# A third pair of raw weight buffers in the feed-forward stages, with two of the four weight sums made in place of raw blocks

## The chip, the cores and the metric

The kernel runs on one core of one Trainium2 chip. The metric is the device time of one execution in microseconds. The core has a matrix engine (TensorE, PE in the profile, with its weight loads as PEld), VectorE (DVE), ScalarE (ACT), GpSimd (POOL), and DMA queues that SyncE (SP) feeds. Each engine works through its own list of instructions in order; between engines an instruction waits on semaphores. TensorE reads its operands from SBUF and adds into PSUM; DVE and ACT read PSUM.

## The reference

The kernel computes two "macaron" layers over T = 528 tokens (16 learned tokens and 512 given ones) of width D = 1024. A layer is a feed-forward half step, a mixer (retention and differential attention) and another feed-forward half step:

```
def swiglu(x, w_gate, w_up, w_down):
    return (jax.nn.silu(x @ w_gate) * (x @ w_up)) @ w_down

for l in range(DEPTH):
    h = h + 0.5 * swiglu(rmsnorm(h, ffn1_norm[l]), ffn1_w_gate[l], ffn1_w_up[l], ffn1_w_down[l])
    proj = rmsnorm(h, mix_norm[l]) @ w_in[l]
    ...
    h = h + jnp.concatenate([y_ret, y_diff], axis=-1) @ w_out[l]
    h = h + 0.5 * swiglu(rmsnorm(h, ffn2_norm[l]), ffn2_w_gate[l], ffn2_w_up[l], ffn2_w_down[l])
return rmsnorm(h, final_norm)[:, N_META:]
```

All of it is in float32, and the inner width of the feed-forward is 2816, that is 22 blocks m of 128.

## The kernel before

**Stages.** The span holds four feed-forward stages, about 30 to 400 us, 700 to 1055, 1055 to 1415 and 1717 to 2094, with a mixer behind the first and behind the third. Each stage is one call of `ffn`, with a pool of SBUF buffers of its own. It works in chunks: the gate and up products of some blocks, then the down projection of those blocks (`FFN_CHUNKS`, `ffn_steps`). The change touches the gate and up products alone.

**Products.** A float32 operand is split into a high part (hi, by ACT, line 108) and the rest (lo, `in - hi`, by DVE, line 109), and each product is made of three matmuls of such parts. The first two blocks of a stage are plain (`plain`; their results leave PSUM on lines 542 and 544). From block 2 on, gate and up of one block are made as one 2x2 Strassen-Winograd product (a "pair"): seven products P1 to P7 of 12 matmuls each, 264 columns wide (256 in the last stage), all issued on line 496. A stage has 20 pairs, the kernel 80.

**Weights of a pair.** Two DMAs bring two raw tiles of 512 KB: `top` (blocks a11, a12) and `bot` (a21, a22). `sums` makes S1 = a21 + a22 (DVE, line 129), S3 = a21 + a11 (DVE, line 130), S2 = S1 + a11 (DVE, line 132) and S4 = S2 + a12 (POOL, line 133), into two tiles `ws0` (S2, S3) and `ws1` (S1, S4). Four splits follow: g1 of `top`, g2 of `ws0`, y of a22 (`yhi`, `ylo`), g3 of `ws1`. The results are named `whi`/`wlo` or `xhi`/`xlo`, by the pool that they lie in. P1 and P2 use g1, P6 and P7 use g2, P5 and P3 use g3, P4 uses y. Raw tiles come from one ring of `RAW_BUFS = 4` tiles (`wraw`), that is two pairs; a DMA into one waits until its last reader is done.

**Results of a pair.** In PSUM, P1, P6, P5 and P3 share bank a of a tile `pm`, P7 and P4 its bank c, P2 lies in a tile `pa`. ACT copies bank a three times (line 455, `rc`): u1 behind P1, u2 behind P6, u4 behind P5. DVE then makes the sums in a tile `gu`: line 469 (P2 + u1), line 474 (bank c + u4, behind P5), lines 476 and 477 (behind P3), line 480 (bank c + u2, behind P4), line 481 (times the gate), and the split of the result into `hh` (ACT, line 551) and `hl` (DVE, line 552). As waits go by the tile, a product waits for every reading of its `pm` tile that stands before it: P6 for the copy u1, P7 for u2, P3 for line 474, P4 for line 476.

**Order.** `rounds` asks for P5(n), P1(m), P2(m), P3(n), P6(m), P4(n), P7(m), n being m - 1, and calls `W.step()` after each for a piece of the next weights. The order in which each engine gets its instructions is then set by a scheduler that runs over the program with a timeline of its own.

Of the kernel before, what the change touches and what calls it, by code (L numbers as in the profile page):

```python
# [8 lines left out]
F32 = mybir.dt.float32  # L9
F32R = mybir.dt.float32r  # L10
AF = mybir.ActivationFunctionType
ALU = mybir.AluOpType
# [3 lines left out]
T = 528  # L16
# [47 lines left out]
class Weights:  # L64


    def __init__(self, nc, pool, plan, ahead, dma_ahead):
        self.nc, self.pool, self.plan = nc, pool, plan
        self.ahead, self.dma_ahead = ahead, dma_ahead
        self.raw, self.parts = {}, {}  # L70
        self.n_dma = self.n_split = self.n_used = 0
        self.extra, self.turn = None, 0
        self.gen, self.hold = None, True

    def raw_tile(self):
        return self.pool.tile([128, 1024], F32, tag="wraw", name="wraw", bufs=RAW_BUFS)

    def start(self):
# [9 lines left out]
    def advance_dma(self, upto):  # L88
        nc = self.nc
        while self.n_dma < min(upto, len(self.plan)):  # L90
            srcs, n, kind = self.plan[self.n_dma]
            self.raw[self.n_dma] = [self.raw_tile() for _ in srcs]
            for t, src in zip(self.raw[self.n_dma], srcs):
                nc.sync.dma_start(out=t[:, :n], in_=src)
            self.n_dma += 1
# [15 lines left out]
    def sums(self, i):  # L111

        nc = self.nc
        self.advance_dma(i + 1)
        top, bot = self.raw.pop(i)
        a11, a12, a21, a22 = (t[:, c] for t in (top, bot) for c in (slice(0, 512), slice(512, 1024)))
        S = [self.extra.tile([128, 2 * 528], F32, tag=f"ws{k}", name=f"ws{k}") for k in range(2)]
        s2, s3, s1, s4 = (t[:, 512 * k:512 * k + 512] for t in S for k in range(2))
        g1 = self.parts_tile(True)
        ops = self.parts[i] = {}  # L120

        def put(names, parts):
            for k, name in enumerate(names):
                ops[name] = tuple(p[:, 512 * k:512 * k + 512] for p in parts)

        self.split(g1, top)
        put(("A11", "A12"), g1)
        yield
        nc.vector.tensor_tensor(out=s1, in0=a21, in1=a22, op=ALU.add)
        nc.vector.tensor_tensor(out=s3, in0=a21, in1=a11, op=ALU.add)  # L130
        yield
        nc.vector.tensor_tensor(out=s2, in0=s1, in1=a11, op=ALU.add)  # L132
        nc.gpsimd.tensor_tensor(out=s4, in0=s2, in1=a12, op=ALU.add)  # L133
        yield
        g2 = self.parts_tile(True)
        self.split(g2, S[0][:, 0:1024])
        put(("S2", "S3"), g2)
        yield
        g4 = [self.extra.tile([128, 528], F32R, tag="y" + p, name="y" + p, bufs=2) for p in ("hi", "lo")]
        self.split([p[:, 0:512] for p in g4], a22)  # L140
        put(("A22",), g4)
        yield
        g3 = self.parts_tile(True)
        self.split(g3, S[1][:, 0:1024])
        put(("S1", "S4"), g3)

    def advance_split(self, upto):
# [59 lines left out]
def trunk(ctx, tc, hT, gains, wgu, wd, win, wout, gnw, sublnw, lam, ret_cs, diff_cs, dtab, mask, out):  # L207
    nc = tc.nc
# [7 lines left out]
    for l in range(DEPTH):  # L216
        for f in range(2):
# [5 lines left out]
            for what, *args in ffn_steps(stage_kind(l, f)):  # L223
                if what == "gu":
                    m, = args
# [208 lines left out]
    def ffn(l, f, mode, g_next, kind):  # L434
        with tc.tile_pool(name=f"ffn{l}{f}", bufs=1, reuse_waits="tile") as pool:
            W.extra, W.turn, W.hold = pool, 3, False
            rr = cols(r, mode)
            w = mode[2] // 2
            state, hidden, room = {}, {}, {}

            def scratch(m):

                if m == "t":
                    return pool.tile([128, 1056], F32, tag="gu", name="xt", bufs=2)
                if m < 4:
                    tag = f"h{'hl'[m % 2]}{6 + m // 2}"
                    return pool.tile([128, T], F32, tag=tag, name=tag)
                i = m // 2 - 2
                if i not in room:
                    room[i] = pool.tile([128, 2 * T], F32, tag=f"ws{i}", name=f"ws{i}")  # L450
                return room[i][:, m % 2 * T:m % 2 * T + T]

            def copy(src):
                t = pool.tile([128, 264], F32, tag="rc", name="rc", bufs=5)[:, :w]
# [121 lines left out]
            def down(ab, final):  # L576
                c0, c1 = ab
                if final:
                    n = KF - 1
                    rounds((("P5", n), ("P3", n), ("P4", n)))  # L580
                    act_table(LNEXP)
                srcs = [hidden.pop(m) for m in range(c0, c1)]
                W.hold = final
                for i, (m, md) in enumerate(down_order(kind, final)):
                    P = project(md, srcs, ("pm", "pa")[i % 2])
                    nc.vector.scalar_tensor_tensor(
                        out=P, in0=P, scalar=0.5, in1=cols(r, md), op0=ALU.mult, op1=ALU.mult
                    )
                    nc.vector.tensor_tensor(out=cols(h[m], md), in0=cols(h[m], md), in1=P, op=ALU.add)
                    if not final:  # L590
                        W.step()
                        continue
                    post_h(m, g_next, md, kind, scratch)
                    if g_next == 3 * DEPTH and m == KD - 1:
                        finish(md)
# [415 lines left out]
    for k in PAIRED:  # L1011
# [8 lines left out]
        out=ident, in_=ident, pattern=[[-1, 128]], compare_op=ALU.is_equal, fill=0.0, base=0,  # L1020
# [12 lines left out]
    for l in range(DEPTH):  # L1033
        last = l == DEPTH - 1
        ffn(l, 0, FULL, 3 * l + 1, "mix")
        if l == 0:
            lambdas()
        mix(l, LAST if last else FULL)
        ffn(l, 1, LAST if last else FULL, 3 * l + 3, "last" if last else "pairs")
# [99 lines left out]
```

## Time and profile before

| what | value |
|---|---|
| time of three runs | 2098.67, 2098.49, 2093.8 us, median 2098.49 us |
| time of the profiled execution | 2096.26 us |
| its span, first to last instruction | 2094.5 us |
| mean granted clock of TensorE | 0.992 |
| TensorE busy | 2006.8 us, 96% |
| DVE busy | 1573.0 us, 75% |
| ACT busy | 965.7 us, 46% |
| POOL busy | 410.0 us, 20% |

TensorE is the engine that nearly always works. What the other engines do shows in the time only where TensorE waits for them. The rows give starts and durations in microseconds; the modelled end of a matmul lies about 0.28 us behind its start, while the starts lie 0.12 us apart, so matmuls overlap in the rows.

### The profile page before, as it was taken

What the parts mean: (1) busy time and instruction counts of PE and PEld (TensorE: products, weight loads), DVE (VectorE), ACT (ScalarE), POOL (GpSimd) and SP (SyncE); (2) the same over time, 40 slices, a digit from 0 to 9 for tenths busy, and PEclk for the clock granted to TensorE, in tenths of its full rate; (3) what the DMA queues carried; (4) which work ended last, traced back from release to release, by engine and by line L of the source; (5) the groups of instructions that cost most, each with busy time, mean ns of one, the idle gap of its engine ahead of it and who ended that gap; (6) DMA issues with size and microseconds to landing.
All of it is one profiled execution on the core that took longest, in us unless ns stands there. A gap on an engine that the chain in (4) does not pass through costs nothing. (4 is left out here: it accounts for less than half of the span.)

```text
span 2094.5 us, 36936 instructions
## 1 busy us (share of the span) xinstructions
PE 2006.8 (96%) x15238; PEld 1930.9 (92%) x15238; DVE 1573.0 (75%) x2292; ACT 965.7 (46%) x1506; POOL 410.0 (20%) x286
## 2 busy tenths in 40 slices
PE   6999999999999999999989999999999999999996
PEld 5899999999999999999989999999888879898995
DVE  8867857668777886867698587766778789696765
ACT  5533525445446552543565254344554465353443
POOL 4100000344343100100110010004434331010002
PEclk8999999999999999999999999999999999999998
DMA  4241323321112242232323223233212223333231
GB/s 153 91 131 52 121 81 95 120 68 64 57 61 90 89 123 70 95 129 68 94 102 102 91 91 116 67 99 114 66 62 62 70 81 101 101 101 121 80 104 49
DMA packets 57656, 190.08 MB, mean 91 GB/s; under 512 B 7056, under 2 KB 9104, under 8 KB 57488
## 3 DMA queue, kind: packets, MB, share of 16 engines
q1 hardware_dynamic: 56464, 186.66, 27.4%
q8 instruction: 119, 1.95, 0.4%
q10 hardware_dynamic: 1024, 1.08, 0.3%
q14 instruction: 49, 0.40, 0.1%
HBM read 184.53 MB, written 2.10 MB: 89 GB/s over the span
## 5 line engine op out<-in xcount | busy, mean ns | idle before, releaser
L133 POOL TENSOR_TENSOR ws<-ws,wraw 128x512 f32<-128x512 f32 x80 | 118.7, 1484 | 1101.0 <-DVE ws L132 931.8
L108 ACT ACTIVATE whi<-wraw 128x1024 fp32r<-128x1024 f32 (+1 forms) x180 | 184.8, 1032 | 274.7 <-PE pm L280 149.2
L496 PE MATMUL pm<-XH,xhi 128*128 128x264 f32 (+1 forms) x848 | 243.2, 287 | 11.0 <-DVE gu L474 5.4
L496 PE MATMUL pm<-XH,xlo 128*128 128x264 f32 (+1 forms) x848 | 240.5, 284 | 0.0
L496 PE MATMUL pm<-XL,xhi 128*128 128x264 f32 (+1 forms) x848 | 240.4, 283 | 0.0
L496 PE MATMUL pm<-XH,whi 128*128 128x264 f32 (+1 forms) x752 | 215.6, 287 | 6.8 <-DVE gu L474 6.6
L496 PE MATMUL pm<-XH,wlo 128*128 128x264 f32 (+1 forms) x752 | 213.1, 283 | 0.0
L496 PE MATMUL pm<-XL,whi 128*128 128x264 f32 (+1 forms) x752 | 213.0, 283 | 0.0
L109 DVE TENSOR_TENSOR wlo<-wraw,whi 128x1024 fp32r<-128x1024 f32 (+1 forms) x148 | 186.2, 1258 | 25.1 <-ACT whi L108 24.4
L280 PE MATMUL pm<-XH,whi 128*128 128x264 f32 (+1 forms) x768 | 181.1, 304 | 9.1 <-DVE ra L668 8.2
L280 PE MATMUL pm<-XL,whi 128*128 128x264 f32 (+1 forms) x768 | 178.7, 301 | 0.0
L280 PE MATMUL pm<-XH,wlo 128*128 128x264 f32 (+1 forms) x768 | 178.7, 302 | 0.0
L496 PEld LDWEIGHTS pm<-XH,xhi 128*128 128x128 f32 x848 | 159.5, 188 | 16.3 <-DVE gu L474 7.9
L496 PEld LDWEIGHTS pm<-XH,xlo 128*128 128x128 f32 x848 | 159.8, 188 | 0.3
L496 PEld LDWEIGHTS pm<-XL,xhi 128*128 128x128 f32 x848 | 159.9, 189 | 0.0
L496 PEld LDWEIGHTS pm<-XH,whi 128*128 128x128 f32 x752 | 141.4, 188 | 9.8 <-DVE gu L474 8.9
L496 PEld LDWEIGHTS pm<-XH,wlo 128*128 128x128 f32 x752 | 141.7, 188 | 0.2
L496 PEld LDWEIGHTS pm<-XL,whi 128*128 128x128 f32 x752 | 141.7, 188 | 0.0
L280 PEld LDWEIGHTS pm<-XH,whi 128*128 128x128 f32 x768 | 123.8, 189 | 16.9 <-issue 4.1
L108 ACT ACTIVATE xhi<-ws 128x1024 fp32r<-128x1024 f32 x84 | 88.9, 1058 | 103.7 <-PE pm L496 37.1
L108 ACT ACTIVATE whi<-ws 128x1024 fp32r<-128x1024 f32 x76 | 80.5, 1059 | 108.9 <-PE pm L496 45.2
L280 PEld LDWEIGHTS pm<-XL,whi 128*128 128x128 f32 x768 | 123.4, 189 | 4.7
(268 smaller groups left out, 6083.6 us busy)
## 6 DMA issues: line engine op xcount, KB each, us to landing
wraw<-in_wgu SPq DMA_DIRECT2D x175, 512.0 KB
wraw<-in_wd SPq DMA_DIRECT2D x66, 512.0 KB
wraw<-in_win SPq DMA_DIRECT2D x56, 512.0 KB
wraw<-in_wd SPq DMA_DIRECT2D x32, 384.0 KB
wraw<-in_wout SPq DMA_DIRECT2D x16, 512.0 KB
slabs<-in_hT SPq DMA_DIRECT2D x8, 264.0 KB
out_y<-slabs SPq DMA_DIRECT2D x8, 256.0 KB
acc1h<-in_dtab SPq DMA_DIRECT2D x4, 264.0 KB
```

Source lines behind the costliest of these rows:

```text
L108: self.nc.scalar.activation(out=hi, in_=t, func=AF.Copy)
L109: (eng or self.nc.vector).tensor_tensor(out=lo, in0=t, in1=hi.bitcast(F32), op=ALU.subtract)
L133: nc.gpsimd.tensor_tensor(out=s4, in0=s2, in1=a12, op=ALU.add)
L280: nc.tensor.matmul(out=ps[:, o:o + c1 - c0], lhsT=a, rhs=b[:, c0:c1], start=start and n == 0, stop=stop and n == 2,)
L496: nc.tensor.matmul(out=out_, lhsT=p[:, s], rhs=q, start=k == 0 and n == 0 and what in ("P1", "P2", "P7"), stop=k == 3 and n == 2, skip_gro ...
```

## The change

Every third pair is fetched into a ring of its own, `xraw`, of two tiles, in the stage's pool. The tiles `ws0` and `ws1` become one tile `ws` (S2, S3). S1 is written over a21 and S4 over a22, both in the raw tile `bot`. So a22 has to be split (y) before S4 overwrites it: `yhi` is issued before the sums and `ylo` ahead of POOL's S4, which now waits for it; and g3 is split from `bot`, which stays in use until then. The number of matmuls, splits, sums and DMAs stays the same. Lines move down by four in most places: 108 becomes 112, 109 becomes 113 (`ylo` 139), 129/130/132/133 become 136/135/138/143, 455 becomes 459, 469/474/476/480/481 become 473/478/480/484/485, 496 becomes 500, 542 becomes 546, 552 becomes 556.

```diff
-    def raw_tile(self):
+    def raw_tile(self, own=False):
+        if own:
+            return self.extra.tile([128, 1024], F32, tag="xraw", name="xraw", bufs=2)
         return self.pool.tile([128, 1024], F32, tag="wraw", name="wraw", bufs=RAW_BUFS)
...
             srcs, n, kind = self.plan[self.n_dma]
-            self.raw[self.n_dma] = [self.raw_tile() for _ in srcs]
+            own = kind == "pair" and self.extra is not None
+            self.n_pairs += own
+            self.raw[self.n_dma] = [self.raw_tile(own and self.n_pairs % 3 == 0) for _ in srcs]
...
-        S = [self.extra.tile([128, 2 * 528], F32, tag=f"ws{k}", name=f"ws{k}") for k in range(2)]
-        s2, s3, s1, s4 = (t[:, 512 * k:512 * k + 512] for t in S for k in range(2))
+        S = self.extra.tile([128, 1024], F32, tag="ws", name="ws")
+        s2, s3 = S[:, 0:512], S[:, 512:1024]
...
         yield
-        nc.vector.tensor_tensor(out=s1, in0=a21, in1=a22, op=ALU.add)
+        g4 = [self.extra.tile([128, 528], F32R, tag="y" + p, name="y" + p, bufs=2) for p in ("hi", "lo")]
+        nc.scalar.activation(out=g4[0][:, 0:512], in_=a22, func=AF.Copy)
         nc.vector.tensor_tensor(out=s3, in0=a21, in1=a11, op=ALU.add)
+        nc.vector.tensor_tensor(out=a21, in0=a21, in1=a22, op=ALU.add)
         yield
-        nc.vector.tensor_tensor(out=s2, in0=s1, in1=a11, op=ALU.add)
-        nc.gpsimd.tensor_tensor(out=s4, in0=s2, in1=a12, op=ALU.add)
+        nc.vector.tensor_tensor(out=s2, in0=a21, in1=a11, op=ALU.add)
+        nc.vector.tensor_tensor(
+            out=g4[1][:, 0:512], in0=a22, in1=g4[0][:, 0:512].bitcast(F32), op=ALU.subtract
+        )
+        put(("A22",), [p[:, 0:512] for p in g4])
+        nc.gpsimd.tensor_tensor(out=a22, in0=s2, in1=a12, op=ALU.add)
         yield
         g2 = self.parts_tile(True)
-        self.split(g2, S[0][:, 0:1024])
+        self.split(g2, S)
         put(("S2", "S3"), g2)
         yield
-        g4 = [self.extra.tile([128, 528], F32R, tag="y" + p, name="y" + p, bufs=2) for p in ("hi", "lo")]
-        self.split([p[:, 0:512] for p in g4], a22)
-        put(("A22",), g4)
-        yield
         g3 = self.parts_tile(True)
-        self.split(g3, S[1][:, 0:1024])
+        self.split(g3, bot)
         put(("S1", "S4"), g3)
```

The scratch tiles of the last down projection, which lay in the `ws` buffers, now lie in those of `yhi` and `ylo`.

The first place is on DVE in the first chunk of the first stage, from the sum behind one pair's P4 (`gu_612`, bank c of `pm_575`) on. Before:

```order
L480 TENSOR_TENSOR gu_612<-pm_575,rc_669 128x264
L481 SCALAR_TENSOR_TENSOR gu_612<-gu_612 128x528
L109 TENSOR_TENSOR ylo_694<-wraw_387,yhi_693 128x512
L552 TENSOR_TENSOR hl3_824<-gu_612,hh3_823 128x528
L109 TENSOR_TENSOR xlo_788<-ws0_734,xhi_787 128x1024
L474 TENSOR_TENSOR gu_752<-pm_713,rc_859 128x264
L130 TENSOR_TENSOR ws0_862<-wraw_578,wraw_577 128x512
```

The same place of the change, where the pair is `gu_618` and the next one `gu_747`:

```order
L484 TENSOR_TENSOR gu_618<-pm_576,rc_673 128x264
L485 SCALAR_TENSOR_TENSOR gu_618<-gu_618 128x528
L139 TENSOR_TENSOR ylo_622<-wraw_386,yhi_621 128x512
L478 TENSOR_TENSOR gu_747<-pm_709,rc_854 128x264
L556 TENSOR_TENSOR hl3_823<-gu_618,hh3_822 128x528
L135 TENSOR_TENSOR ws_730<-wraw_502,wraw_501 128x512
L473 TENSOR_TENSOR gu_874<-pa_839,rc_875 128x264
L136 TENSOR_TENSOR wraw_502<-wraw_502 128x512
L481 TENSOR_TENSOR gu_874<-gu_874,r_71 128x264
L480 TENSOR_TENSOR gu_747<-pm_709,r_71 128x264
L113 TENSOR_TENSOR wlo_676<-wraw_386,whi_675 128x1024
```

The sum behind P5 (line 474, now 478) stood behind a 1024-wide split and now stands right behind `ylo`. The raw tile `bot` of this pair (`wraw_387`, now `wraw_386`) was read for the last time by `ylo_694`, and is now read until `wlo_676`.

The second place is the pair after that one. On DVE the change has there:

```order
L484 TENSOR_TENSOR gu_747<-pm_709,rc_802 128x264
L139 TENSOR_TENSOR ylo_751<-wraw_502,yhi_750 128x512
L485 SCALAR_TENSOR_TENSOR gu_747<-gu_747 128x528
L113 TENSOR_TENSOR xlo_787<-ws_730,xhi_786 128x1024
L556 TENSOR_TENSOR hl4_950<-gu_747,hh4_949 128x528
L478 TENSOR_TENSOR gu_874<-pm_838,rc_981 128x264
L135 TENSOR_TENSOR ws_857<-xraw_579,xraw_578 128x512
L113 TENSOR_TENSOR xlo_805<-wraw_502,xhi_804 128x1024
```

POOL's S4 into `wraw_502` may start behind `ylo_751`. On ACT at that place, before:

```order
L455 ACTIVATE rc_987<-pm_843 128x264
L108 ACTIVATE xhi_992<-wraw_715 128x1024
L455 ACTIVATE rc_1009<-pm_971 128x264
L108 ACTIVATE whi_955<-ws1_863 128x1024
L266 ACTIVATE gu_880<-gu_880 128x528
L455 ACTIVATE rc_1059<-pm_971 128x264
```

And on ACT in the change, where the next pair's tile is `pm_965`:

```order
L459 ACTIVATE rc_981<-pm_838 128x264
L112 ACTIVATE xhi_804<-wraw_502 128x1024
L112 ACTIVATE xhi_985<-wraw_711 128x1024
L459 ACTIVATE rc_1002<-pm_965 128x264
L459 ACTIVATE rc_1056<-pm_965 128x264
L272 ACTIVATE gu_874<-gu_874 128x528
```

The copy u1 (`rc_1009`) stood ahead of the split that reads S4 (`whi_955`); now u1 (`rc_1002`) stands behind that split (`xhi_804`) and another.

The third place is the start of the first stage on DVE, around the results of the two plain blocks (`gu` on line 542, now 546). Before:

```order
L413 SCALAR_TENSOR_TENSOR r_71<-sq_265,sq_266 128x528
L109 TENSOR_TENSOR wlo_450<-ws0_403,whi_449 128x1024
L542 TENSOR_TENSOR gu_349<-pm_207,r_71 128x528
L542 TENSOR_TENSOR gu_485<-pm_361,r_71 128x528
L109 TENSOR_TENSOR wlo_482<-ws1_404,whi_481 128x1024
L130 TENSOR_TENSOR ws0_522<-wraw_358,wraw_357 128x512
```

And in the change:

```order
L113 TENSOR_TENSOR wlo_452<-ws_402,whi_451 128x1024
L419 SCALAR_TENSOR_TENSOR r_71<-sq_265,sq_266 128x528
L113 TENSOR_TENSOR wlo_468<-wraw_275,whi_467 128x1024
L135 TENSOR_TENSOR ws_520<-xraw_357,xraw_356 128x512
L546 TENSOR_TENSOR gu_348<-pm_207,r_71 128x528
L546 TENSOR_TENSOR gu_483<-pm_360,r_71 128x528
```

A split of g3 (`wlo_482`, now `wlo_468`) and the first sum of the third pair moved ahead of the two results; the split of g2 (`wlo_450`, now `wlo_452`) moved ahead of line 413, now 419.

## Rows read from the trace of the kernel before

**Rows 1.** The page, busy time of TensorE.
```profile
PE 2006.8 (96%) x15238; PEld 1930.9 (92%) x15238; DVE 1573.0 (75%) x2292; ACT 965.7 (46%) x1506; POOL 410.0 (20%) x286
```
**Rows 2.** Waits of PE: waiting line, whom for: us in total, times, longest.
```profile
PE pm L496 <- DVE gu L474: 12.0, 16, 1.7
...
PE pm L496 <- DVE gu L476: 4.0, 7, 0.9
PE pm L496 <- DVE gu L542: 3.7, 2, 2.0
PE pa L496 <- DVE gu L469: 3.1, 3, 1.5
...
PE pm L496 <- ACT rc L455: 1.3, 5, 0.3
```
**Rows 3.** Timeline of PE around one such wait: start, duration, instruction, idle before.
```profile
100.42 0.28 PE L496 MATMUL pm<-XL,xhi 128*128 128x264 f32 x1
101.09 0.39 PE L496 MATMUL pm<-XH,whi 128*128 128x264 f32 x1 [0.39 <-DVE gu L474]
101.32 0.28 PE L496 MATMUL pm<-XH,wlo 128*128 128x264 f32 x1
```
**Rows 4.** PE by windows: us, busy (matmuls), clock, DMA share, GB/s.
```profile
200.00:250.00 50.00, 48.86 (x388) 1.00 0.30 106
250.00:300.00 50.00, 50.00 (x414) 1.00 0.37 117
```
**Rows 5.** Timeline of DVE, first stage, first chunk.
```profile
89.74 0.43 DVE L474 TENSOR_TENSOR gu<-pm,rc 128x264 f32<-128x264 f32 x1
...
96.37 0.43 DVE L480 TENSOR_TENSOR gu<-pm,rc 128x264 f32<-128x264 f32 x1 [0.56 <-PE pm L496]
96.91 0.90 DVE L481 SCALAR_TENSOR_TENSOR gu<-gu 128x528 f32<-128x528 f32 x1
97.73 0.68 DVE L109 TENSOR_TENSOR ylo<-wraw,yhi 128x512 fp32r<-128x512 f32 x1
98.52 0.71 DVE L552 TENSOR_TENSOR hl<-gu,hh 128x528 fp32r<-128x528 f32 x1
99.47 1.23 DVE L109 TENSOR_TENSOR wlo<-ws,whi 128x1024 fp32r<-128x1024 f32 x1 [0.24 <-ACT whi L108]
100.61 0.43 DVE L474 TENSOR_TENSOR gu<-pm,rc 128x264 f32<-128x264 f32 x1
```
**Rows 6.** That chunk: PE, PEld, DVE, ACT, POOL busy, then as above.
```profile
78.00:110.00 32.00, 29.87 (x241) 29.45 (x242) 28.45 (x43) 16.59 (x26) 3.87 (x3) 1.00 0.29 95
```
**Rows 7.** Waits of DVE for weights.
```profile
DVE ws L130 <- DMA wraw<-in_wgu: 32.3, 29, 3.4
```
**Rows 8.** Timeline of DVE, first stage, second chunk.
```profile
203.74 0.69 DVE L130 TENSOR_TENSOR ws<-wraw 128x512 f32<-128x512 f32 x1 [1.52 <-DMA wraw<-in_wgu]
...
209.19 1.71 DVE L109 TENSOR_TENSOR ylo<-wraw,yhi 128x512 fp32r<-128x512 f32 x1
```
**Rows 9.** Timeline of PE around a copy u2.
```profile
180.89 0.28 PE L496 MATMUL pa<-XH,whi 128*128 128x264 f32 x1
181.41 0.39 PE L496 MATMUL pm<-XH,xhi 128*128 128x264 f32 x1 [0.23 <-ACT rc L455]
```
**Rows 10.** Timeline of DVE at the first stage's start.
```profile
53.73 1.31 DVE L542 TENSOR_TENSOR gu<-pm,r 128x528 f32<-128x528 f32 x2
56.06 1.23 DVE L109 TENSOR_TENSOR wlo<-ws,whi 128x1024 fp32r<-128x1024 f32 x1 [1.02 <-ACT whi L108]
57.20 0.68 DVE L130 TENSOR_TENSOR ws<-wraw 128x512 f32<-128x512 f32 x1
```
**Rows 11.** Timeline of POOL: S4 near 51 us, and in the second chunk.
```profile
51.16 3.78 POOL L133 TENSOR_TENSOR ws<-ws,wraw 128x512 f32<-128x512 f32 x1 [8.70 <-DVE ws L132]
...
209.06 1.29 POOL L133 TENSOR_TENSOR ws<-ws,wraw 128x512 f32<-128x512 f32 x1 [9.49 <-DVE ws L132]
```
**Rows 12.** Timeline of ACT: one 1024-wide high part.
```profile
102.92 1.06 ACT L108 ACTIVATE whi<-ws 128x1024 fp32r<-128x1024 f32 x1 [0.84 <-PE pm L496]
```

More of the change, by code (lines that the diff above doesn't have):

```diff
@@ L71, in __init__ @@
         self.n_dma = self.n_split = self.n_used = 0
-        self.extra, self.turn = None, 0
+        self.extra, self.turn, self.n_pairs = None, 0, 0
         self.gen, self.hold = None, True
-    def raw_tile(self):
+    def raw_tile(self, own=False):
+        if own:
+            return self.extra.tile([128, 1024], F32, tag="xraw", name="xraw", bufs=2)
         return self.pool.tile([128, 1024], F32, tag="wraw", name="wraw", bufs=RAW_BUFS)
@@ L438, in ffn @@
             w = mode[2] // 2
-            state, hidden, room = {}, {}, {}
+            state, hidden = {}, {}
             def scratch(m):
@@ L447, in scratch @@
                     return pool.tile([128, T], F32, tag=tag, name=tag)
[L448 to L451, printed above, removed]
+                tag = "y" + ("hi", "lo")[m % 2]
+                return pool.tile([128, T], F32, tag=tag, name="xb", bufs=2)
             def copy(src):
```

## The prediction

> **What bounds the kernel now.** I read the page's busy times first, then the waits of TensorE, then single waits in the timelines, then what VectorE does in the same stretch. TensorE is busy for 2006.8 of 2094.5 us [rows 1], so a change can only win back what TensorE loses by waiting, and can only cost where it makes TensorE wait. The change touches the gate and up products, line 496. There TensorE waits 12.0 us for line 474 (sixteen times, ahead of P3), 4.0 for line 476 (seven times, ahead of P4), 3.7 for line 542 (twice, at stage starts), 3.1 for line 469 (three times) and 1.3 for the copies on line 455 (five times) [rows 2]. That is 24.1 us in 33 waits.
>
> A shown wait is less than what it costs. Undisturbed, 414 matmuls start in 50 us, one each 0.121 us [rows 4]. Around a wait shown as 0.39 us the starts lie 0.67 and then 0.23 us apart [rows 3]; against 0.121 each that loses 0.55 and 0.11, together 0.66, so 0.27 more than is shown. With 33 x 0.27 = 8.9 the ceiling of what can come back is 33.0 us. The windows say the same in the rough: a window of the second chunk has 388 matmuls instead of 414 [rows 4], 3.2 us lost in 50.
>
> **VectorE is nearly as full as TensorE in these stretches.** From 78 to 110 us it is busy for 28.45 of 32 us [rows 6]. A pair takes 100.61 - 89.74 = 10.87 us there [rows 5], so VectorE works 9.66 us per pair. TensorE's 84 matmuls need 10.2. VectorE has about half a microsecond to spare per pair, and everything depends on what stands where in its list.
>
> **Line 474 moves up.** In the first chunk line 480 starts behind P4 at 96.37, and then 481, `ylo`, `hl` and a split of 1.14 us (99.47 to 100.61) stand ahead of line 474, which ends at 101.04 [rows 5]; P3 should have started at 100.42 + 0.12 [rows 3]. The change puts 478 right behind `ylo` in one pair of two (first place in the order): by the starts of the same rows it then begins 98.52 - 96.37 = 2.15 us behind line 484's start and ends after 2.6, where 28 matmuls, 3.4 us, now stand between P4 and P3 in TensorE's list. In the next pair (second place) the split and `hl` are still ahead of it, which takes some 3.8 us and 0.43 for itself, but 47 matmuls, 5.7 us, stand there. So both kinds of pair have 0.8 us or more in hand. These sixteen waits cost 12.0 + 16 x 0.27 = 16.3 us. I take back 13, since the first pair of each stage stays tight. Bounds: 0, if other lateness fills the gap, and 16.3.
>
> **The weights no longer come late.** VectorE waits 32.3 us for raw weights on line 130 [rows 7], in the second chunks of every stage above all. At 203.74 it has stood for 1.52 us [rows 8], and lines 469 and 476 queue behind it, for which P2's and P4's banks wait. Before, `bot` is in use for 24 rows of VectorE's list, from line 130 to `ylo`, with two pairs of buffers. Now it is 15 rows, to the low part of g3, with three. The DMA then starts at least one pair earlier, 10 us, against a wait that is at most 3.4 us long [rows 7]. The waits on lines 476 and 469 cost 4.0 + 3.1 + 10 x 0.27 = 9.8 us, of which I take back 8. Bounds: 0 and 9.8.
>
> **P7 directly behind P6.** P7 must wait for the copy u2 of P6's result. In the order of before P7 stands directly behind P6 (with fewer than three other matmuls between) in 4 of 80 pairs, in the change in 17. Such a place reads 180.89 to 181.41 [rows 9], 0.52 us where 0.12 is due, with 0.1 behind it as above, so 0.5 us. 13 x 0.5 = +6.5. It costs nothing where TensorE would have waited just after anyway, so the bounds are 0 and +6.5.
>
> **The first stage starts later.** Line 546 now stands behind one more split, 57.20 - 56.06 = 1.14 us, and behind line 135, 0.68 us [rows 10]. That is 1.8 us, and up to 1.0 more if the split waits for ACT as it did at 56.06 [rows 10]. TensorE waits for this line already [rows 2], so all of it counts: +2. The other three stages have no more work ahead of that line. Bounds: 0 and +2.8.
>
> **S4 meets VectorE.** At 209.06 POOL's S4 runs for 1.29 us [rows 11], and `ylo`, which starts in it, takes 1.71 us [rows 8] instead of 0.68 [rows 5]: 1.03 us lost on VectorE. Now S4 is released by the end of `ylo`, so in nearly every pair the next sum or split of VectorE with two SBUF operands can lose this. That hurts where 478 is still to come behind it, in the 15 or so pairs ordered like the second place. They have about a microsecond in hand, so I count a third of a microsecond for each: +5. Bounds: 0, and 80 x (1.03 - 0.5 to spare) = +42.
>
> **Sum.** -13 - 8 + 6.5 + 2 + 5 = -7.5 us. The profiled execution took 2096.26 us, so 2088.8. The median of the runs shown, 2098.49, lies 2.2 us higher; I leave the prediction at **2089 us**. A difference within 0.3% of the median (6.3 us, so from 2092.2 to 2104.8) can hardly be told from no change.
>
> **Rival 1, VectorE becomes the limit (no measurable change).** If S4 takes 1.03 us from VectorE in every pair, of which before has some already (0.90 on line 481, where `hl`, as wide, takes 0.71 [rows 5], so 0.2), VectorE needs 9.66 + 0.8 = 10.5 us per pair against 10.2. Then line 478 comes late although it stands earlier, the 13 us stay lost, and only the weights' 8 come back: 2096.3 - 8 + 6.5 + 2 = 2097 us. For it speaks that the lock is seen in the trace; against it, that a PSUM reading operation, 478, often stands right behind `ylo`, and that VectorE's list has slack in the chunks that no longer wait for weights. The Trainium skill, "SBUF — State Buffer", section "🔬 SBUF: two separate sides", says that VectorE and GpSimd share a port pair as an exclusive lock, held for a whole instruction by whichever starts first, with VectorE operations on two SBUF operands among those that need it. The 1.71 us agree with it.
>
> **Rival 2, the gains without the costs (clearly faster).** If u2's copy and the collisions fall into time that TensorE had to spare, and the first pairs gain too: 2096.3 - 16.3 - 9.8 + 2 = 2072 us.
>
> **Rival 3, S4 is starved and a copy comes late (slower).** Near 51 us S4 took 3.78 us [rows 11], while VectorE ran operations on SBUF back to back until line 542, at 53.73 [rows 10], which reads PSUM. At the second place `ylo` is followed by three such operations without a break until 478. There ACT has `xhi_804`, which reads S4, then another split, each 1.06 us [rows 12], ahead of the copy u1, for which P6 waits. P6 stands 59 matmuls, 7.2 us, behind P4. `ylo` ends about 1.3 us behind P4, or 2.3 if VectorE runs a microsecond late; the splits and the copy take 2.5; so S4 has 3.4 or 2.4 us. At 1.29 nothing happens; at 3.78 P6 waits up to 1.3 us. In 15 pairs this costs 20 us and brings -13 - 8 + 6.5 + 2 + 20 = +7.5, 2104 us; with ten more pairs in which g3's parts come late for P5 it is 2117. Against it: S4 usually took 1.29 us.
>
> **Rival 4, the weights still come late.** A DMA into `xraw` has the same queue as all others, and one that waits for its buffer holds the next. Then the 8 us do not come, nor, with VectorE late, half of the 13: 2096.3 - 6.5 + 6.5 + 2 + 5 = 2103 us. Against it: 10 us of lead against 3.4.
>
> **Chances.** My forecast 0.42 (2081 to 2094, of which 0.38 is faster by over 0.3%), rival 1 0.23 (0.03 faster, 0.18 the same, 0.02 slower), rival 2 0.15 (faster), rival 3 0.13 (slower), rival 4 0.07 (0.05 the same, 0.02 slower). So faster 0.56, same 0.27, slower 0.17. The range goes from below rival 2, 2068, to rival 4 and the mild end of rival 3, 2104. The forecast's own range is 2081 to 2094.
>
> **What would show it.** Right: VectorE's waits for raw weights at line 135 near 0; the waits on 478 below 4 us and on 480 and 473 below 2; some 18 waits on the copies of line 459 with 6 us in all as lost; the first line 546 about 2 us later. Wrong: many waits on line 459 of a microsecond, ahead of P6, with S4 above 2.5 us (rival 3); waits on 478 as many as before, with VectorE without pauses (rival 1); waits for DMA on line 135 (rival 4).

## The result, and the profile after

The changed kernel takes 2122.45 us (median of 4 runs, 2121.13 to 2124.05) against 2098.58 us before: a ratio of 1.0114, 95% interval 1.0099 to 1.013. It is 24 us slower, where 2089 us had been forecast. The profiled execution took 2122.54 us, 26.3 us more than the one before, and its span is 2120.5 us.

The page's busy times, and POOL's S4 in the view of groups by line (busy time, mean of one, idle before and what ended it):

```profile
PE 2018.9 (95%) x15238; PEld 1940.5 (92%) x15238; DVE 1565.0 (74%) x2292; ACT 961.6 (45%) x1506; POOL 449.1 (21%) x286
...
L143 POOL TENSOR_TENSOR wraw<-ws,wraw 128x512 f32<-128x512 f32 x54 | 107.2, 1985 | 772.2 <-DVE ylo L139 572.1 <-DVE ws L138 168.5 <-ACT hh L555 26.2
L143 POOL TENSOR_TENSOR xraw<-ws,xraw 128x512 f32<-128x512 f32 x26 | 50.3, 1934 | 356.4 <-DVE ylo L139 328.3 <-PE pa L522 18.5 <-DVE ws L138 9.6
```

The 80 S4 take 107.2 + 50.3 = 157.5 us of POOL, 1.97 us each, where before they took 118.7 us, 1.48 each. Eighteen of them last over 2.6 us (before, four).

TensorE's waits in the changed kernel, of the gate and up products (line 500) and of the down projection (286), to be read beside [rows 2]:

```profile
PE pm L500 <- ACT rc L459: 16.7, 27, 2.8
...
PE pm L500 <- DVE gu L546: 7.9, 2, 6.3
PE pm L500 <- DVE gu L478: 7.2, 7, 1.3
...
PE pa L500 <- DVE xlo L113: 2.9, 6, 0.9
PE pa L286 <- ACT whi L112: 2.5, 3, 0.9
...
PE pa L500 <- ACT whi L112: 1.6, 4, 0.6
...
PE pm L500 <- DVE gu L480: 0.7, 1, 0.7
PE pa L500 <- ACT xhi L112: 0.6, 1, 0.6
PE pa L286 <- DVE xlo L113: 0.6, 1, 0.6
```

With the 0.27 us that a wait costs beyond what is shown, the account is:

| TensorE waits for | before | after | difference | forecast |
|---|---|---|---|---|
| line 474, now 478 | 12.0 + 16 x 0.27 = 16.3 | 7.2 + 7 x 0.27 = 9.1 | -7.2 | -13 |
| 476 and 469, now 480 and 473 | 9.8 | 0.7 + 0.27 = 1.0 | -8.8 | -8 |
| the copies, 455, now 459 | 1.3 + 5 x 0.27 = 2.7 | 16.7 + 27 x 0.27 = 24.0 | +21.3 | +6.5 and +5 |
| 542, now 546 | 3.7 + 0.5 = 4.2 | 7.9 + 0.5 = 8.4 | +4.2 | +2 |
| parts of weights, for P2 and the down projection | 0.7 + 0.3 = 1.0 | 8.2 + 15 x 0.27 = 12.3 | +11.3 | none |

That is +20.8 us of the 26.3. About 2 more are the lower clock at the start, shown below. Two single waits of before that are gone, on line 544 and of tile `pa` for a copy, gave back 1.8 us and aren't in the table, so some 5 us are left without an account.

The mechanism can be read at one place, the second one of the order lists in the section on the change. VectorE's timeline there (start, duration, instruction, idle before and what ended it):

```profile
101.65 0.42 DVE L484 TENSOR_TENSOR gu<-pm,rc 128x264 f32<-128x264 f32 x1
101.99 0.67 DVE L139 TENSOR_TENSOR ylo<-wraw,yhi 128x512 fp32r<-128x512 f32 x1
102.59 0.69 DVE L485 SCALAR_TENSOR_TENSOR gu<-gu 128x528 f32<-128x528 f32 x1
103.21 1.21 DVE L113 TENSOR_TENSOR xlo<-ws,xhi 128x1024 fp32r<-128x1024 f32 x1
104.35 0.69 DVE L556 TENSOR_TENSOR hl<-gu,hh 128x528 fp32r<-128x528 f32 x1
104.97 0.42 DVE L478 TENSOR_TENSOR gu<-pm,rc 128x264 f32<-128x264 f32 x1
106.23 0.69 DVE L135 TENSOR_TENSOR ws<-xraw 128x512 f32<-128x512 f32 x1 [0.84 <-POOL wraw L143]
```

POOL's timeline, this S4 and two others:

```profile
49.70 5.87 POOL L143 TENSOR_TENSOR wraw<-ws,wraw 128x512 f32<-128x512 f32 x1 [5.38 <-ACT XH L333]
...
102.80 3.39 POOL L143 TENSOR_TENSOR wraw<-ws,wraw 128x512 f32<-128x512 f32 x1 [6.74 <-DVE ylo L139]
...
125.08 3.88 POOL L143 TENSOR_TENSOR wraw<-ws,wraw 128x512 f32<-128x512 f32 x1 [6.74 <-DVE ylo L139]
```

ACT's timeline, and then TensorE's, behind that S4 (two 1024-wide high parts stand in one row):

```profile
103.87 0.37 ACT L459 ACTIVATE rc<-pm 128x264 f32<-128x264 f32 x1
106.22 2.01 ACT L112 ACTIVATE xhi<-wraw 128x1024 fp32r<-128x1024 f32 x2 [1.98 <-POOL wraw L143]
108.14 0.37 ACT L459 ACTIVATE rc<-pm 128x264 f32<-128x264 f32 x1
```

```profile
107.63 0.28 PE L500 MATMUL pm<-XL,whi 128*128 128x264 f32 x1
108.56 0.39 PE L500 MATMUL pm<-XH,xhi 128*128 128x264 f32 x1 [0.64 <-ACT rc L459]
...
130.38 0.39 PE L500 MATMUL pm<-XH,xhi 128*128 128x264 f32 x1 [2.84 <-ACT rc L459]
```

S4 is released when `ylo` ends, 102.66, and starts at 102.80. VectorE's next three operations (485, a split, `hl`) read two SBUF operands each and follow one another without a gap. S4 ends at 106.19, which is 1.22 us behind the start of 478, the first operation that reads PSUM; alone it takes 1.29. ACT has waited 1.98 us for it, makes two splits, and only then the copy u1, for which P6 waits at 108.56. The S4 of 125.08 does the same, with 2.84 us at TensorE. At 97.73 in [rows 5] `ylo` waited for nothing of that kind, since S4 had started behind line 132, with a pause and then 480, which reads PSUM, next on VectorE.

Counted by the starts of all matmuls (start to start less 0.12 us, from 0.1 us on), the waits of tile `pm` that a copy ended cost TensorE 2.7 us in 7 places before and 23.1 in 37 after. In 15 places it is P6 that waits for u1, and ACT's work ahead of that copy begins with the end of an S4; these cost 11.2 us, of which two cost 3.0 each (before, no such place). In 18 places P7 waits for u2, mostly directly behind P6; these cost 10.1 us (before, 4 with 1.7). The other 4 cost 1.8. The copies are not all that S4 holds up: waits of `pa` for parts of weights that lead back to the end of an S4 through ACT's and VectorE's lists cost another 9.8 us in 21 places (before, none).

The start of the first stage, VectorE's timeline (to be read beside [rows 10]), and TensorE by windows:

```profile
52.62 1.21 DVE L113 TENSOR_TENSOR wlo<-ws,whi 128x1024 fp32r<-128x1024 f32 x1
53.76 0.69 DVE L419 SCALAR_TENSOR_TENSOR r<-sq 128x528 f32<-128x528 f32 x1
56.69 1.23 DVE L113 TENSOR_TENSOR wlo<-wraw,whi 128x1024 fp32r<-128x1024 f32 x1 [2.24 <-ACT whi L112]
57.83 0.68 DVE L135 TENSOR_TENSOR ws<-xraw 128x512 f32<-128x512 f32 x1
58.43 1.31 DVE L546 TENSOR_TENSOR gu<-pm,r 128x528 f32<-128x528 f32 x2
```

```profile
56.00:59.00 3.00, 0.00 (x0) 0.78 0.78 265
59.00:62.00 3.00, 2.72 (x12) 0.50 0.70 270
62.00:66.00 4.00, 4.00 (x26) 0.69 0.00 0
```

Line 546 starts at 58.43 instead of 53.73. TensorE waits 6.3 us, and then the granted clock is 0.50, the 1.2 GHz level, and 0.69 in the next window: 38 matmuls start in 7 us, where 58 fit at 0.121 us.

### The profile page after: what moved, and what is told of

Its sections match the earlier page's. It is cut to its first block, busy times and chain, and to the rows that moved or that the text cites. A ratio compares the mean times of both kernels' runs of the same rounds, so it can differ in the third digit from the quotient of the medians.

```text
span 2120.5 us, 36818 instructions
## 1 busy us (share of the span) xinstructions
PE 2018.9 (95%) x15238; PEld 1940.5 (92%) x15238; DVE 1565.0 (74%) x2292; ACT 961.6 (45%) x1506; POOL 449.1 (21%) x286
## 3 DMA queue, kind: packets, MB, share of 16 engines
q10 hardware_dynamic: 1024, 1.08, 0.3%
## 5 line engine op out<-in xcount | busy, mean ns | idle before, releaser
L112 ACT ACTIVATE whi<-wraw 128x1024 fp32r<-128x1024 f32 (+1 forms) x196 | 199.8, 1033 | 273.1 <-PE pm L286 131.4
L143 POOL TENSOR_TENSOR wraw<-ws,wraw 128x512 f32<-128x512 f32 x54 | 107.2, 1985 | 772.2 <-DVE ylo L139 572.1
L113 DVE TENSOR_TENSOR wlo<-wraw,whi 128x1024 fp32r<-128x1024 f32 (+1 forms) x164 | 203.4, 1244 | 29.0 <-ACT whi L112 28.5
L459 ACT ACTIVATE rc<-pm 128x264 f32<-128x264 f32 (+1 forms) x240 | 90.9, 381 | 144.8 <-PE pm L500 144.4
L500 PEld LDWEIGHTS pm<-XL,whi 128*128 128x128 f32 x752 | 142.3, 189 | 0.0
L590 DVE SCALAR_TENSOR_TENSOR pm<-pm,r 128x528 f32<-128x528 f32 (+2 forms) x49 | 34.2, 698 | 130.8 <-PE pm L286 130.8
L112 ACT ACTIVATE xhi<-wraw 128x1024 fp32r<-128x1024 f32 (+1 forms) x98 | 99.7, 1028 | 68.5 <-DMA wraw<-in_wd 17.0
```

The costliest lines, as they stand in the source:

```text
L112: self.nc.scalar.activation(out=hi, in_=t, func=AF.Copy)
L113: (eng or self.nc.vector).tensor_tensor(out=lo, in0=t, in1=hi.bitcast(F32), op=ALU.subtract)
L143: nc.gpsimd.tensor_tensor(out=a22, in0=s2, in1=a12, op=ALU.add)
L459: nc.scalar.activation(out=t, in_=src, func=AF.Copy)
L500: nc.tensor.matmul(out=out_, lhsT=p[:, s], rhs=q, start=k == 0 and n == 0 and what in ("P1", "P2", "P7"), stop=k == 3 and n == 2, skip_gro ...
L590: nc.vector.scalar_tensor_tensor(out=P, in0=P, scalar=0.5, in1=cols(r, md), op0=ALU.mult, op1=ALU.mult)
```

## The experiments

Theory A: S4 is released by `ylo`, is starved by VectorE's run of operations, and ACT, which takes its list in order, brings the copies late. Theory B: the loss comes with the third pair of buffers, its transfers and its order. Every kernel here gets a new order from the scheduler; the runs that move only a few S4 change it least.

**The sums in place, without the third pair of buffers.**

```diff
-            self.raw[self.n_dma] = [self.raw_tile(own and self.n_pairs % 3 == 0) for _ in srcs]
+            self.raw[self.n_dma] = [self.raw_tile(own and False) for _ in srcs]
```

> The change without its third pair of buffers: S1 and S4 are made in place, every pair is fetched into the old ring of four raw tiles. Theory A (S4 is now released by the end of ylo, finds VectorE in a run of operations on SBUF, and ACT, waiting for S4 in order, brings the copies for P6 and P7 late): slow like the change, 2115 to 2135 us, S4 above 2.6 us in 10 or more pairs, TensorE's waits on the copies 12 us or more; and VectorE's waits for raw weights as before or longer, since the lower raw tile is held longer. Theory B (the loss comes with the third pair of buffers, by its transfers and the order that they bring): near before, 2095 to 2103 us, waits on the copies below 5 us.

2117.01 us, ratio 1.0079 (1.0055 to 1.0103). Slow without the third pair, which rules out B as the main cause. S4 lasts over 2.6 us in 12 pairs, as A has it, but the copies cost 6.1 us in 14 waits, not 12; more of the loss lies at split weights and line 480 (5.3 us in 8 waits). The third pair makes it 5 us slower still in the change; line 546 of the first stage, which the change brings at 58.43, starts at 53.88 here.

**One extra buffer, no sum in place.** On the kernel before:

```diff
+        if own:
+            return self.extra.tile([128, 1024], F32, tag="xraw", name="xraw", bufs=1)
...
+            self.raw[self.n_dma] = [self.raw_tile(own and k == 1 and self.n_pairs % 2 == 0) for k in range(len(srcs))]
```

(The `ws` tiles are 1024 wide, and the scratch tiles lie in `yhi` and `ylo` as in the change, so that it fits.)

> The other half: no sum in place, S4 as before, but the lower raw tile of every second pair comes into one extra buffer of the stage's pool (two extra ones don't fit beside the two weight-sum tiles). Theory A: not slower than before, 2088 to 2099 us; S4 1.3 us in most pairs, waits on the copies near 1.3 us in all; VectorE's waits for raw weights fall from 32 us to below 15. Theory B: slower than before by 10 us or more, 2108 to 2125 us.

2091.69 us, ratio 0.996 (0.9947 to 0.9973): faster than before by 0.4%, where B had it slower. S4 is over 2.6 us in 4 pairs, as before. VectorE's waits for raw weights there, and then the second line of them that the kernel before has beside [rows 7]:

```profile
DVE ws L134 <- DMA wraw<-in_wgu: 28.2, 8, 3.6
DVE ws L134 <- DMA xraw<-in_wgu: 14.2, 13, 1.7
```

```profile
DVE ws L129 <- DMA wraw<-in_wgu: 10.9, 7, 1.8
```

These did not fall below 15 us as expected; they stayed, at 42.4 us in 21 waits against 32.3 + 10.9 = 43.2 in 36 before. TensorE's waits on 474 and 476 (lines 476 and 478 here) still fell, from 16.0 to 10.8 + 3.5 = 14.3 us. So a wait of VectorE for a transfer is worth what stands behind it, and its sum says little.

**S4 on VectorE, in all pairs.** In the change:

```diff
-        nc.gpsimd.tensor_tensor(out=a22, in0=s2, in1=a12, op=ALU.add)
+        nc.vector.tensor_tensor(out=a22, in0=s2, in1=a12, op=ALU.add)
```

> The change, with S4 on VectorE instead of POOL, so that no lock is left between the two in these stages; VectorE has 80 x 0.61 = 49 us more work. Theory A: no wait of ACT on POOL, TensorE's waits on the copies fall from 16.7 us to below 6, the first stage starts 3 to 4 us earlier; as VectorE is then nearly full, 2098 to 2115 us. Theory B: the loss stays and VectorE's new work comes on top, 2125 us or more.

2099.93 us, ratio 1.0007 (0.9996 to 1.0018): 22 us of the change's 24 are gone, with 80 more operations on VectorE. In time A holds, B doesn't. The copies did not follow, where A had them below 6 us: TensorE waits 16.2 us for them, in 35 waits of at most 1.4 us. Only three places lead back to an S4 any more, 0.4 us each; by the starts 26 are P7 waiting for u2 (15.2 us), in an order that has more of that. What fell are the waits of `pa` for parts (8.2 us in 15 waits to 1.4 in 5), those on line 478 (7.2 to 4.8) and on 546 (7.9 to 6.0). So this run doesn't show the step by way of the copies.

**The sums in place of the upper tile**, so that S4 doesn't wait for `ylo`:

```diff
-        nc.vector.tensor_tensor(out=a21, in0=a21, in1=a22, op=ALU.add)
+        nc.vector.tensor_tensor(out=s2, in0=s3, in1=a22, op=ALU.add)
         yield
-        nc.vector.tensor_tensor(out=s2, in0=a21, in1=a11, op=ALU.add)
+        nc.vector.tensor_tensor(out=a11, in0=a21, in1=a22, op=ALU.add)
...
-        nc.gpsimd.tensor_tensor(out=a22, in0=s2, in1=a12, op=ALU.add)
+        nc.gpsimd.tensor_tensor(out=a12, in0=s2, in1=a12, op=ALU.add)
...
-        self.split(g3, bot)
+        self.split(g3, top)
```

> The change with the sums made in place of the upper raw tile: S3 = a21 + a11, S2 = S3 + a22, then S1 over a11 and S4 over a12, so that S4 doesn't wait for ylo (the sum S2 is added in another order). Buffers as in the change. S4 is released behind S1, a split ahead of the sum behind P4. Theory A: S4 stays below 2.6 us in nearly all pairs and the copies stand ahead of the split that reads S4; waits on the copies below 5 us, 2088 to 2102 us. Theory B: as slow as the change, 2112 to 2128 us.

2092.31 us, ratio 0.9963 (0.995 to 0.9977). With the same buffers and the same number of operations as the change it is 30 us faster than that. S4 is over 2.6 us in 6 pairs. The copies cost 7.1 us in 12 waits, more than the 5 expected.

**One S4 of 80 on VectorE**, that of 49.70 us (`self.n_sums` counts the pairs):

```diff
+        eng = nc.vector if self.n_sums - 1 in ON_DVE else nc.gpsimd
+        eng.tensor_tensor(out=a22, in0=s2, in1=a12, op=ALU.add)
...
+ON_DVE = (1,)
```

> The change, with one single S4 of 80 on VectorE: that of the first stage's second pair, which took POOL 5.87 us. On the engines' lists nothing else moves but one ylo. Theory A (S4 starved, ACT and VectorE behind it): the first line 546 comes 2 to 3 us earlier, TensorE doesn't fall to its lower clock there, and the whole is 4 to 6 us faster than the change, 2116 to 2119 us. Rival (the start is late because a split and a sum stand ahead of line 546, whatever S4 does): 2121 to 2123 us.

2123.13 us, ratio 1.012 (1.0096 to 1.0144): no gain that could be told within the intervals, the rival's figure (the span of the profiled execution is 1.5 us below the change's). VectorE's timeline says why:

```profile
54.95 0.69 DVE L422 SCALAR_TENSOR_TENSOR r<-sq 128x528 f32<-128x528 f32 x1
55.57 1.21 DVE L113 TENSOR_TENSOR wlo<-wraw,whi 128x1024 fp32r<-128x1024 f32 x1
56.70 0.68 DVE L135 TENSOR_TENSOR ws<-xraw 128x512 f32<-128x512 f32 x1
57.30 1.31 DVE L549 TENSOR_TENSOR gu<-pm,r 128x528 f32<-128x528 f32 x2
```

The wait of 2.24 us for ACT is gone, but VectorE comes to it 1.2 us later, and the result of the first block is read at 57.30 (line 549 here), 1.1 us earlier than in the change and 3.6 later than before. The granted clock from 59 to 62 us is 0.55 here too, behind a pause of 4.6 us, though it is 1.00 from 62 us on, where the change had 0.69. So the late start is, for its larger part, the list: what stands ahead of 546.

**The 18 long S4 on VectorE, and, as a control, 18 short ones.** The same edit with ON_DVE = (1, 4, 6, 12, 14, 19, 24, 26, 32, 34, 39, 44, 52, 54, 59, 64, 70, 78), all over 2.6 us in the change, or (2, 5, 7, 10, 13, 15, 22, 25, 27, 31, 33, 38, 45, 51, 53, 55, 61, 66), all at most 1.30.

> The change, with the 18 S4 on VectorE that took POOL over 2.6 us, the one above among them; 62 stay on POOL. Theory A: ACT waits for POOL in the gate and up products for less than 30 us instead of 47, the losses of TensorE behind S4 (11 us) and the late start (6 us) go, 2101 to 2109 us. Rival (the loss is spread over all pairs, or comes from the new order): 2116 us or more.

> The control: the change, with 18 other S4 on VectorE, all of which took POOL 1.28 to 1.30 us. Theory A: no gain, 2117 to 2127 us. If the gain of the run before comes from less work on POOL or a different order as such, this one is as fast as that, 2101 to 2110 us.

The long ones: 2107.86 us, ratio 1.0045 (1.0031 to 1.0059). The short ones: 2120.26 us, ratio 1.0105 (1.0083 to 1.0126). So 18 operations of 0.68 us moved to the busier engine bring 0.7% of the time, 14.6 us against the change's 2122.45, or 0.8 us each, and 18 others bring 0.1%, which is within the intervals. ACT's waits for S4, in the change first and then with the long ones on VectorE:

```profile
ACT whi L112 <- POOL wraw L143: 18.7, 13, 4.4
...
ACT xhi L112 <- POOL wraw L143: 13.8, 11, 2.2
ACT whi L112 <- POOL xraw L143: 8.0, 6, 2.2
...
ACT xhi L112 <- POOL xraw L143: 6.4, 4, 2.2
```

```profile
ACT whi L112 <- POOL wraw L145: 7.7, 6, 3.0
...
ACT whi L112 <- POOL xraw L145: 4.2, 5, 1.9
...
ACT xhi L112 <- POOL wraw L145: 3.4, 6, 0.9
ACT xhi L112 <- POOL xraw L145: 2.2, 2, 1.6
```

46.9 us become 17.5, with 8.9 more for the S4 on VectorE. TensorE's waits for the copies there:

```profile
PE pm L503 <- ACT rc L462: 12.2, 26, 1.0
```

They fell by 4.5 us, from 16.7, and the longest from 2.8 to 1.0. By the starts, the copies behind an S4 cost 3.1 us instead of 11.2, the others 15.3 instead of 11.9, and the parts behind an S4 cost 3.0 instead of 9.8. The late start, which A had going too, stayed for the most part: TensorE waits 6.4 us for the results of the plain blocks, against 7.9. So the time shows what the long S4 cost; of its 14.6 us, 4.5 came back at the copies.

At the place shown above VectorE does the same work in less time, with S4 among it:

```profile
101.07 1.21 DVE L113 TENSOR_TENSOR xlo<-ws,xhi 128x1024 fp32r<-128x1024 f32 x1
102.20 0.68 DVE L145 TENSOR_TENSOR wraw<-ws,wraw 128x512 f32<-128x512 f32 x1
102.81 0.69 DVE L559 TENSOR_TENSOR hl<-gu,hh 128x528 fp32r<-128x528 f32 x1
103.42 0.42 DVE L481 TENSOR_TENSOR gu<-pm,rc 128x264 f32<-128x264 f32 x1
103.77 0.67 DVE L135 TENSOR_TENSOR ws<-xraw 128x512 f32<-128x512 f32 x1
```

S4 is done at 102.88, 3 us after the start of `ylo` (99.85), instead of 4.2 (106.19 after 101.99), and line 135 follows the first sum behind P5 (481 here, 478 in the change) at once. In the change it had waited 0.84 us for POOL, since it writes the tile `ws`, which S4 reads.

**The upper tile, without the third pair of buffers** (the first edit, on the kernel with the sums in the upper tile).

> The sums in place of the upper raw tile, without the third pair of buffers: shows what the buffers are worth where S4 isn't starved. Theory A with late weights worth some 8 us: 2096 to 2104 us, VectorE's waits for raw weights back at 20 to 35 us. If the buffers bring nothing: 2089 to 2095 us, as with them.

2114.59 us, ratio 1.0076 (1.0055 to 1.0097), far above both figures. VectorE's waits for raw weights there, and with the third pair:

```profile
DVE ws L135 <- DMA wraw<-in_wgu: 38.7, 31, 3.8
```

```profile
DVE ws L135 <- DMA wraw<-in_wgu: 11.9, 6, 3.7
```

With the sums in the upper tile the third pair is worth 22 us. Not all of it need be the transfers, since the order changed as well (TensorE waits 5.3 us for one line 546). Without the third pair the choice of the tile hardly counts: 2114.59 us in the upper one, 2117.01 in the lower, with intervals that overlap.

**The long S4 on VectorE in two more kernels.** In the one without the third pair 12 of them, (1, 12, 14, 19, 32, 34, 39, 52, 54, 59, 70, 78); in the one with the upper tile 6, (10, 22, 30, 41, 50, 62).

> The sums in place without the third pair of buffers, with the 12 S4 on VectorE that took POOL over 2.6 us there. Theory A: as with the 18 of the change, which brought 0.8 us for each, some 6 to 12 us less than with all on POOL, 2105 to 2111 us; the rest above before is late weights and P7 behind P6. Rival (here the loss is late weights alone): 2114 us or more.

> The sums in place of the upper raw tile, with the third pair of buffers, and the 6 S4 on VectorE that took POOL over 2.6 us. Theory A: 2 to 5 us less than with all on POOL, 2087 to 2091 us. Rival (the few long S4 left lie where nothing waits for them): 2091 to 2094 us.

The first: 2105.48 us, ratio 1.0028 (1.0017 to 1.0039), down from 1.0079, which is 11 us or 0.9 for each. In time that is as A has it, but not by way of the copies: TensorE waits 6.1 us for them in 14 waits, with the S4 moved and without. What fell are waits of `pa` for high parts of weights, `whi`, from 7.4 us in 10 waits to 1.8 in 3. The second: 2093.45 us, ratio 0.9967 (0.9955 to 0.9979), not different from 0.9963: there the rival is right, the few long S4 left hold up nothing.

**The upper tile, with the two extra buffers for the upper tile of every second pair.**

> The sums in place of the upper raw tile, where the two extra buffers take the upper tile of every second pair instead of both tiles of every third: as the upper tile is now the one held long, weights come even earlier. If late weights still cost there: 2086 to 2091 us, with VectorE's waits for raw weights below 10 us. If they cost nothing any more, the order alone decides: 2089 to 2097 us.

2098.67 us, ratio 0.9994 (0.9984 to 1.0004). Neither: it loses the gain, and VectorE's waits for raw weights are 28.9 us in 10 waits. Whether these or the new order did it wasn't separated.

## Why the prediction was wrong

**The step that failed** is "S4 meets VectorE", the +5 of the sum. It took S4 at 1.29 us and looked for the loss on VectorE (1.03 us of an operation that waits for POOL). The runs show the other side of the same lock: S4 loses, 18 times for 2.7 to 5.9 us, and ACT, more than VectorE, carries the loss on, to the copies (11.2 us in 15 places) and to parts of weights (9.8 us in 21). Moving these 18 gave back 14.6 us. At the copies this was rival 3, with its place, its chain and its condition (S4 longer than 2.4 to 3.4 us) as written, and with a chance of 0.13 that was far too low. The row of 3.78 us near 51 us [rows 11] had shown what a run of SBUF operations does to S4, and the order list showed such a run behind `ylo` in some fifteen pairs. Against it I held that "S4 usually took 1.29 us"; but in the kernel before, an operation that reads PSUM stood right behind S4's release in 56 of 80 pairs, in the change in 22. The usual duration belonged to an order that the change had taken away. Rival 3's price, 20 us for 15 pairs at the copies, was too high for these, 11.2 us. That the time still came out above its 2104 us lies, by the account, in other terms: the parts (which it had late for P5 alone), line 474, which gave back less, and the start.

**P7 directly behind P6**: right in kind and number (18 waits for u2 where 17 places were counted), somewhat small in size: +6.5 forecast, which was also its upper bound, 10.1 - 1.7 = 8.4 by the starts. It wasn't tested by itself.

**The first stage's start**: the direction was right, the size wrong. Forecast +2 (at most 2.8); line 546 comes 4.7 us later (58.43 against 53.73). Its two operations ahead were counted, and at most 1.0 us for a split that waits for ACT; it waits 2.24, since ACT waits for a starved S4. The lower clock after TensorE's longer pause had no term. With that one S4 elsewhere the total didn't measurably fall and the result still came 3.6 us late, so most of this loss is the list.

**Line 474**: mis-sized, -13 forecast, -7.2 by the waits. Seven waits are left, the longest of 1.3 us.

**Late weights**: right in size. Lines 476 and 469 gave back 8.8 us where 8 were forecast, and VectorE's waits on raw weights at line 135 fell from 32.3 to 9.7 us, though not to near 0; without the third pair they were already down to 20.3. The single extra buffer by itself brings 0.4%, some 8 us, with VectorE's waits for weights as long as before, so that run doesn't show that earlier weights were what helped.

**What no term had**: P2 and the down projection waiting for parts of weights, 11.3 us. Of these the waits of tile `pa` for `whi` (1.6 us at line 500, 2.5 at 286) fall to 0 and 0.4 us when the long S4 lie on VectorE, so they were S4's too; those for `xlo` (2.9) stay, 1.6 us for `wlo` at 289 (286 in the change) come new, and neither was tried by itself.

**Rival 1**, with VectorE as the limit, had the rule of the Trainium skill's page "SBUF — State Buffer", section "🔬 SBUF: two separate sides", for its mechanism: an exclusive lock that a VectorE operation on two SBUF operands or a POOL operation holds for its whole length, whichever starts first. The trace of the change agrees with the lock: `hl`, which reads two SBUF operands and takes 0.69 us at 104.35, takes 1.42 where the S4 of 125.08 runs until 128.96.

```profile
128.10 1.42 DVE L556 TENSOR_TENSOR hl<-gu,hh 128x528 fp32r<-128x528 f32 x1
```

The rival's outcome didn't come, since VectorE was less busy than before (1565.0 against 1573.0 us).

The 9 us that the kernel with the long S4 on VectorE still lies above before (ratio 1.0045) fit the start and P7 behind P6, less the gains; that is argued from the account, not shown by a run.

## What to carry to other kernels

An operation's usual duration holds for the instructions that stood around it. When a change moves what releases a GpSimd operation, look at what VectorE has right behind the release: here, three operations on SBUF in a row made 1.3 us into 3.4, and the engine that waited next brought it to TensorE. Follow every wait that hangs on such an operation, not only the one that was foreseen: of the 14.6 us that moving the long S4 gave back, 4.5 came back at the copies. Where a buffer is reused in place, it can count which half is overwritten: with the third pair of buffers, the same sums over the upper raw tile were 30 us faster than over the lower one, and faster than the kernel before; without it there was no clear difference.

## What the runs showed of the hardware

At the places shown, GpSimd didn't get in between VectorE's operations on SBUF while these followed one another without a gap. S4's end lies 1.22 us (106.19) behind the start of the first operation that reads PSUM, at 104.97, and in the longest case, 5.87 us, 1.12 us behind the end of line 419 (54.45), with VectorE idle after it. In other places it does get in: before, at 209.06, it started while an operation that reads PSUM ran, and the one that waited was `ylo`, 1.71 us.

TensorE's granted clock stayed at 1.00 over the pause before 54.6 us in the kernel before (waits of 2.0 us on line 542), and stood at 0.50 from 59 to 62 us behind the pause of 6.3 us in the change. In the window from 66 to 72 us it was 1.00 again.
